# Row-wise log-softmax: stores moved to a second DMA queue, loads issued up to seven tiles ahead

## The chip, the cores and the metric

One core of one Trainium2 chip. The metric is the device time of one execution in microseconds (us), on the slowest core, which here is the only one. The granted clock was 1.0 in the profile of every run, and all runs were in the fast state.

## The reference

```python
x = randn(16, 512, 50000), float32
max_x = max(x, axis=-1);  shifted = x - max_x
out = shifted - log(sum(exp(shifted), axis=-1))
```

8192 rows of 50,000 numbers: 1638.4 MB are read once and 1638.4 MB written once.

## The kernel before

A tile is 16 whole rows, each cut into 8 pieces, so 128 partitions of 6250 numbers (25,000 B). There are 512 tiles and 8 buffers. A tile is loaded, reduced, exponentiated for its sum, scaled in place and stored from the same buffer.

```python
NBUF = 8
AHEAD = 5
...
    def load(t):
        buf = data.tile([P, W], FP32, name="buf")
        nc.sync.dma_start(out=buf, in_=xt[t])            # L75
...
    def front(t):
        nc.vector.reduce_max(out=pmax, in_=buf, axis=AX)  # L81
        ...                                  # row maximum over the 8 pieces -> negmax
        for j in range(nexp):                # 2 x 3125 columns, exp and its sum, L102
            nc.scalar.activation(out=dump, ..., func=ACT.Exp, bias=negmax[:, 0:1],
                                 accum_out=part[:, j : j + 1])
        ...                                  # TensorE sums the 8 pieces (L108), ScalarE takes Ln
    def back(t):
        nc.vector.tensor_scalar(out=buf, in0=buf, ...)    # L117, in place
        nc.sync.dma_start(out=ot[t], in_=buf)             # L121

    for t in range(AHEAD):
        load(t)
    for t in range(ntiles + 1):
        if t + AHEAD < ntiles:
            load(t + AHEAD)
        if t < ntiles:
            front(t)
        if t >= 1:
            back(t - 1)
```

The instructions of each engine run in the order of the program. Load k takes the buffer of tile k-8 and so waits for store k-8 to land, in this kernel and in the changed one.

## Time and profile before

| | before |
|---|---|
| time, median of 3 runs | 7904.5 us (7893.95 to 7905.24) |
| bytes moved | 3276.8 MB, 414 GB/s over the span |
| DMA busy share of its queue | 99.9% |
| VectorE busy | 5566.8 us (70%) |
| ScalarE busy | 3152.9 us (40%) |
| load, issue to landing | 23.5 us |
| store, issue to landing | 30.7 us |

Read the busy share with care. It says that DMA is the bound, not that DMA runs at its best: the share is 1.00 in the stage at 431 GB/s and in the stage at 406 alike. The GB/s row beside it is what tells the two apart. The prediction shows its lines.

### The profile page before, as it was taken

What the parts mean: (1) busy time and instruction counts of PE and PEld (TensorE: products, weight loads), DVE (VectorE), ACT (ScalarE), POOL (GpSimd) and SP (SyncE); (2) the same over time, 40 slices, a digit from 0 to 9 for tenths busy, and PEclk for the clock granted to TensorE, in tenths of its full rate; (3) what the DMA queues carried; (4) which work ended last, traced back from release to release, by engine and by line L of the source; (5) the groups of instructions that cost most, each with busy time, mean ns of one, the idle gap of its engine ahead of it and who ended that gap; (6) DMA issues with size and microseconds to landing.
All of it is one profiled execution on the core that took longest, in us unless ns stands there. A gap on an engine that the chain in (4) does not pass through costs nothing.

```text
span 7908.9 us, 12333 instructions
## 1 busy us (share of the span) xinstructions
PE 600.4 (8%) x2048; PEld 513.0 (6%) x2048; DVE 5566.8 (70%) x3072; ACT 3152.9 (40%) x2561; POOL 1.2 (0%) x7
## 2 busy tenths in 40 slices
PE   0000000000000000000000000000000000000000
PEld 0000000000000000000000000000000000000000
DVE  8777777777777776766666666766666666766665
ACT  4444444444444444333343434333343434333333
POOL 0000000000000000000000000000000000000000
DMA  9999999999999999999999999999999999999999
GB/s 416 426 430 431 431 431 431 431 431 431 431 430 431 429 428 410 410 403 409 409 406 403 404 405 408 407 408 405 409 408 401 406 403 413 408 405 406 406 405 385
DMA packets 147536, 3277.65 MB, mean 414 GB/s; under 512 B 16384, under 2 KB 16384, under 8 KB 16384
## 3 DMA queue, kind: packets, MB, share of 16 engines
q1 hardware_dynamic: 147456, 3276.87, 99.9%
q14 instruction: 64, 0.52, 0.0%
q8 instruction: 16, 0.26, 0.0%
HBM read 1638.40 MB, written 1638.40 MB: 414 GB/s over the span
## 4 chain that ended last, share of the span: by engine, by line
DMA 97%; SPq 1%; DVE 1%; issue 0%; ACT 0%; PE 0%; ACTq 0%
DMA out_dram<-buf 97%; SPq L75 1%; DVE pmax L81 1%; DMA buf<-in_x_dram 0%; DVE buf L117 0%; ACT dump L102 0%; DVE allmax L84 0%; DVE rowmax L86 0%; DVE spread L91 0%; DVE negmax L96 0%; PE rowsum L108 0%; ACT logsum L112 0%; ACTq L102 0%
## 5 line engine op out<-in xcount | busy, mean ns | idle before, releaser
L81 DVE TENSOR_REDUCE pmax<-buf 128x1 f32<-128x6250 f32 x512 | 3411.6, 6663 | 2231.9 <-DMA buf<-in_x_dram 2231.9
L102 ACT ACTIVATE dump<-buf,negmax 128x3125 f32<-128x3125 f32 x1024 | 2937.9, 2869 | 4370.9 <-DVE negmax L96 4354.4
L117 DVE TENSOR_SCALAR buf<-buf,negmax,logsum 128x6250 f32<-128x6250 f32 x512 | 1789.8, 3496 | 4.5 <-ACT logsum L112 3.6
L108 PE MATMUL rowsum<-part,ones 128*128 128x1 f32 x2048 | 600.4, 362 | 7269.8 <-ACT dump L102 7269.8
L108 PEld LDWEIGHTS rowsum<-part,ones 128*128 128x128 f32 x2048 | 513.0, 311 | 7357.1 <-ACT dump L102 7335.3
L112 ACT ACTIVATE logsum<-rowsum 128x1 f32<-128x1 f32 x512 | 87.8, 171 | 345.8 <-PE rowsum L108 345.8
L102 ACT ACTIVATION_READ_ACCUMULATOR dump<-buf,negmax 128x1 f32 x1024 | 190.8, 186 | 0.0
L96 DVE STREAM_TRANSPOSE negmax<-spread 128x32 f32<-128x32 f32 x512 | 108.2, 211 | 17.7
L84 DVE STREAM_TRANSPOSE allmax<-pmax 128x32 f32<-128x32 f32 x512 | 108.2, 211 | 17.5
L86 DVE TENSOR_REDUCE rowmax<-allmax 128x4 f32<-128x32 f32 x512 | 95.3, 186 | 17.8
L91 DVE COPY spread<-rowmax 128x32 f32<-128x32 f32 x512 | 92.9, 181 | 17.8
L67 ACT ACT_TABLE_LOAD x1 | 1.3, 1283 | 0.8 <-PEq L146 0.8
L59 POOL TENSOR_SCALAR_AFFINE_SELECT ones<-ones 128x128 f32<-128x128 f32 x1 | 0.4, 403 | 0.1
L63 POOL TENSOR_SCALAR_AFFINE_SELECT ones<-ones 128x128 f32<-128x128 f32 x1 | 0.4, 398 | 0.1
L57 POOL MEMSET ones<- 128x128 f32 x1 | 0.2, 204 | 0.3 <-POOLq L146 0.3
L146 POOL MEMSET const-bfloat16-1.0<- 128x1 bf16 x1 | 0.1, 102 | 0.0
L146 POOL MEMSET const-uint8-127<- 128x1 uint8 x1 | 0.1, 102 | 0.0
L146 POOL MEMSET const-float32-0.0<- 128x1 f32 x1 | 0.1, 99 | 0.3 <-issue 0.3
L146 POOL MEMSET const-float32-1.0<- 128x1 f32 x1 | 0.1, 99 | 0.0
## 6 DMA issues: line engine op xcount, KB each, us to landing
buf<-in_x_dram SPq DMA_DIRECT2D x512, 3125.0 KB, 23.5
out_dram<-buf SPq DMA_DIRECT2D x512, 3125.0 KB, 30.7
```

The lines of the kernel that those rows point to most:

```text
L59: nc.gpsimd.affine_select(out=ones3, in_=ones3, pattern=[[-G, R], [0, G]], base=0, channel_multiplier=1, compare_op=ALU.is_ge, fill=0.0,)
L67: nc.scalar.preload_act_table_set("natural_log_exp_and_others")
L75: nc.sync.dma_start(out=buf, in_=xt[t])
L81: nc.vector.reduce_max(out=pmax, in_=buf, axis=AX)
L84: nc.vector.transpose(out=allmax, in_=pmax.to_broadcast([P, SQ]))
L86: nc.vector.tensor_reduce(out=rowmax, in_=allmax.rearrange("p (r g) -> p r g", g=G), op=ALU.max, axis=AX, negate=True,)
L91: nc.vector.tensor_copy(out=spread.rearrange("p (r g) -> p r g", g=G), in_=rowmax[:, :, None].to_broadcast([P, SQ // G, G]),)
L96: nc.vector.transpose(out=negmax, in_=spread)
L102: nc.scalar.activation(out=dump, in_=buf[:, j * EXP_C : (j + 1) * EXP_C], func=ACT.Exp, bias=negmax[:, 0:1], scale=1.0, accum_out=part[:, ...
L108: nc.tensor.matmul(rowsum, ones, part[:, j : j + 1], start=j == 0, stop=j == nexp - 1)
L112: nc.scalar.activation(out=logsum, in_=rowsum, func=ACT.Ln)
L117: nc.vector.tensor_scalar(out=buf, in0=buf, scalar1=shift.pop(t)[:, 0:1], scalar2=logs.pop(t), op0=ALU.add, op1=ALU.subtract,)
```

## The change

The intent is that a load waiting for its buffer shall not hold up stores that are ready, and that loads run as far ahead as the buffers allow.

```diff
-AHEAD = 5
+AHEAD = 7
...
-        nc.sync.dma_start(out=ot[t], in_=buf)
+        nc.scalar.dma_start(out=ot[t], in_=buf)
...
     for t in range(ntiles + 1):
-        if t + AHEAD < ntiles:
-            load(t + AHEAD)
         if t < ntiles:
             front(t)
         if t >= 1:
             back(t - 1)
+        if t + AHEAD < ntiles:
+            load(t + AHEAD)
```

## The prediction

> **What bounds the kernel now.** I read the page from the slices down, then the waits, then a stretch of the timeline, then the trace's landing records. The slices first:
>
> ```profile
> DMA  9999999999999999999999999999999999999999
> GB/s 416 426 430 431 431 431 431 431 431 431 431 430 431 429 428 410 410 403 409 409 406 403 404 405 408 407 408 405 409 408 401 406 403 413 408 405 406 406 405 385
> ...
> q1 hardware_dynamic: 147456, 3276.87, 99.9%
> ...
> DMA 97%; SPq 1%; DVE 1%; issue 0%; ACT 0%; PE 0%; ACTq 0%
> ```
>
> The 16 DMA engines are busy 99.9% of the time and the chain that ended last is 97% DMA. So this is a transfer-bound kernel, and only two things can make it shorter: fewer bytes (the change moves the same 3276.87 MB) or more bytes per busy microsecond. The GB/s row is the clue: the same loop runs at 431 GB/s for fourteen slices and at some 406 for the rest. The table by stages says the same and clears the engines: DVE work stays about 69 to 73% busy, waiting in both.
>
> ```profile
> 1000.00:2000.00 1000.00, 78.74 (x269) 67.22 (x269) 728.63 (x402) 414.45 (x336) 0.00 (x0) 1.00 1.00 431
> 3400.00:4400.00 1000.00, 73.88 (x252) 63.11 (x252) 690.57 (x384) 388.95 (x316) 0.00 (x0) 1.00 1.00 406
> ```
>
> (Columns: length, busy us of PE, PEld, DVE, ACT, POOL; clock; DMA share; GB/s.) Who holds the DMA back? The queue's own waits, then one period of the timeline:
>
> ```profile
> SPq L75 <- DMA out_dram<-buf: 7333.8, 504, 23.6
> ```
>
> ```profile
> 1503.27 3.49 DVE L117 TENSOR_SCALAR buf<-buf,negmax,logsum 128x6250 f32<-128x6250 f32 x1
> 1503.29 0.33 SPq L75 DMA_DIRECT2D buf<-in_x_dram  x1
> 1503.66 0.46 SPq L121 DMA_DIRECT2D out_dram<-buf  x1
> 1510.60 6.66 DVE L81 TENSOR_REDUCE pmax<-buf 128x1 f32<-128x6250 f32 x1 [3.83 <-DMA buf<-in_x_dram]
> ```
>
> SyncE stands 7333.8 of 7908.9 us in front of a load, waiting for an old store to free its buffer. It is one in-order queue, so the next store stands behind that load: counting the scaling instructions (L117) done at each store issue, two later tiles are always already scaled when a store goes out. Those are buffers idle in SBUF. What is left in flight when a load is issued is only one load and one store, some 14.8 us of transfer.
>
> Now the part no view prints, from the trace's packets and its 16 landings per DMA (one per DMA engine). A 25,000 B row takes an engine 928 ns in both stages at the median; the loss is a tail. In the 500 us from 1500 us the mean packet is 931 ns, in those from 5000 us 983 ns, with 10% over 1.09 us. The long packets come in bursts that hit nearly all engines within 2 us. The gap from a DMA's first to its last landing, by tile: 1.2 us at the start, 4.6 at tile 20, 8.2 at 80, 11.7 at 140, 11.8 at 180, 13.5 from 220 to the end. One engine falls behind steadily, and at tile 300 the other fifteen lie within 2.6 us of each other with the last one 11.4 us behind them. A load's first landing comes 13.9 us after its issue at tile 100, but only 10.5 us at tiles 150 to 490; the very first load, into empty queues, takes 9.4 us. So from tile 150 on the leading engines have about 1 us of work left when the next load comes. That load needs the slowest engine's old store. The fifteen fast ones pile up at the end of their queue, restart together on every issue and change from load to store together, and then the bursts come. The same collective burst is there from 50 us on, when all engines are still in step from the start (411 GB/s at 60:80), and it fades as they drift apart. In between, spread out but not starved, nothing is lost.
>
> **What the Trainium skill says.** "DMA: Bandwidth & Descriptors", section "Where 436 GB/s comes from": 435 GB/s is the fabric's ceiling. The trace's 431 agrees; there is no room above the first stage. Section "Issuing engines are not separate DMA queues": queues of different issuers run on the same 16 engines and only issue time is saved. On that alone the change would be worth nothing; the trace of before has one busy queue, so cannot confirm it. Section "Queues, rings and completion order": each DMA engine round-robins between the queue rows that have work, packet by packet. If so, loads and stores will alternate row by row on each engine instead of eight rows of one and eight of the other; no run here shows it yet. Section "Latency and other measured facts": copies on the sync and scalar queues reach 214 GB/s per direction at full rate. That is 428 in total, within 1% of the 431 here, and speaks against a toll for alternating queues.
>
> **The change part by part.** Bytes, DMA count and all compute instructions stay.
> - Store issue moves from SyncE to ScalarE: 512 x 0.46 us = 235 us of ScalarE sequencer time. Per tile ScalarE has 2 x 2.87 + 2 x 0.19 + 0.17 = 6.3 us, and with the issue 6.8 of a 14.9 us period. Not on the path. The store follows the Ln of the next tile in program order; in the early timeline Ln ends 6.9 us after negmax and L117 3.4 us after it, so a store goes out some 3.5 us after it is ready. Against a queue tens of us deep that is hidden.
> - Stores no longer stand behind a waiting load. This removes the two scaled idle tiles. It does not remove the 7333.8 us of load wait: load t+7 now waits for store t-1, whose buffer it takes, and SyncE will still stand there nearly all the time.
> - AHEAD 7 with 8 buffers. At the issue of load t+7, a tile is held by compute from its landing until the next tile has landed (14.9 us), that one's maximum (6.66) and the small steps and exps (about 7.8): 29 us, two buffers. My estimate is that the other six are in DMA, as about two stores and four loads. Before the load counted in, that is five transfers x 7.4 = 37 us of backlog instead of 14.8.
> - What 37 us buys: the laggard lost 11.7 us over 140 tiles, 2100 us, so 5.6 ns per us. At that pace it needs 6600 us to drain the leaders, against 2200 before. The bunching then would come, if at all, at the very end. And if the engines do bunch, packet-wise alternation means no common change of direction. Both point the same way.
> - The sum: in the clean stage a tile takes 14.91 us by the slowest engine's landings (tiles 100 to 190), in the late stage 15.75 (250 to 490). All clean is 512 x 14.91 = 7633 us, plus about 10 us for first latency and the last tile's compute that no transfer covers: 7643. A few us of remaining bursts: 7650, or 3.2% below 7904.5.
>
> **Rivals.**
> 1. Hidden anyway. DMA is at 99.9% and the skill says that queues don't add bandwidth; if the 406 comes from addresses in HBM or from mere load/store mixing, the time stays at 7850 to 7950. For: busy share is full in both stages. Against: at tiles 50 to 180 the engines are already spread over most of a load and a store, so mixed, at 431; and the start shows the same bursts at other addresses, when in step.
> 2. A new bunching. With six tiles in DMA the slow engine still gates every load; if the fast ones starve earlier than my backlog says (for instance because the store queue runs dry and half of the loads are withheld), the late stage only starts later. At half of the lossy stage saved: 7904 - 130 = 7775, just within 2%.
> 3. A toll per change of queue. Sixteen changes per tile and engine instead of two. If each cost 50 ns, 16 x 0.05 x 512 = 410 us: 8050. For: in step, a common change costs about 0.5 us. Against: spread engines change direction with no loss in the clean stage (931 ns mean), and at the start the engines are already staggered over 0.8 us, nearly a whole packet.
> 4. ScalarE's in-order stores delaying exps: it has 8 us spare per tile, so I give this little.
>
> **Range and chances.** The floor is 1024 x 7.41 us (eight packets of 925 ns start to start and a 6 ns completion) = 7585, plus ends: not under 7595. The main case gives 7620 to 7700, rival 2 up to 7800, rival 1 up to 7930. I take 7650, with 7605 to 7910 for 8 in 10. Main case with part of rival 2: 0.66 for faster by over 2% (below 7746); rivals 1 and the rest of 2: 0.26 within 2%; rival 3: 0.08 slower.
>
> **What would show each step.** Two hardware queues with about half the bytes each; the GB/s row at 427 to 432 from the second slice to the 38th, with no step down; packets over 1 us nearly gone; in the landing records, a laggard allowed to fall over 20 us behind; SyncE still waiting for stores some 7000 us, but load and store landing times of about 40 to 70 and 20 to 40 us instead of 23.5 and 30.7, as the backlog is deeper; ScalarE waiting for L117 close to never. I am wrong in the mechanism if the row still falls to 406 in mid-run, if packets are longer everywhere, or if DMA share drops below 0.98, which would mean that the queues run dry.

## The result, and the profile after

| | before | after |
|---|---|---|
| time, median of 4 runs each | 7904.87 us (7893.95 to 7924.88) | 7614.22 us (7613.93 to 7616.07) |
| ratio of the fast runs | 1 | 0.963 (0.9611 to 0.9649) |
| GB/s over the span | 414 | 430 |
| load, issue to landing | 23.5 us | 51.9 us |
| store, issue to landing | 30.7 us | 37.5 us |

Ratios here are the mean time of one kernel's fast runs over that of the other's in the same rounds, so not quite the ratio of the medians. The change makes the kernel 3.7% faster. That lies inside the predicted range of 7605 to 7910 us but near its fast end: 36 us below the point forecast of 7650, and 6 us below the main case of 7620 to 7700.

The slices and the queues of the changed kernel:

```profile
DMA  9999999999999999999999999999999999999998
GB/s 425 433 432 432 432 432 432 432 432 432 432 432 432 432 432 432 432 432 432 432 432 432 432 432 432 432 432 432 432 432 432 432 432 432 431 432 432 432 432 380
...
q1 hardware_dynamic: 73728, 1638.43, 50.0%
q10 hardware_dynamic: 73728, 1638.43, 50.0%
```

The DMA row is what it was. The GB/s row has lost its step from 431 to some 406: it stands at 431 to 433 from the second slice to the last but one. Loads (q1) and stores (q10) share the DMA engines equally. The same two stages that the prediction compared, in the table by stages (columns as there), show DVE and ACT working at the same pace in both:

```profile
1000.00:2000.00 1000.00, 78.60 (x268) 67.17 (x268) 732.92 (x408) 413.22 (x336) 0.00 (x0) 1.00 1.00 432
3400.00:4400.00 1000.00, 79.20 (x270) 67.67 (x270) 729.10 (x403) 414.06 (x338) 0.00 (x0) 1.00 1.00 432
```

One period of the timeline, and SyncE's longest wait:

```profile
3001.49 0.34 ACTq L121 DMA_DIRECT2D out_dram<-buf  x1
3001.89 6.66 DVE L81 TENSOR_REDUCE pmax<-buf 128x1 f32<-128x6250 f32 x1 [3.83 <-DMA buf<-in_x_dram]
...
3009.41 3.50 DVE L117 TENSOR_SCALAR buf<-buf,negmax,logsum 128x6250 f32<-128x6250 f32 x1
```

```profile
SPq L75 <- DMA out_dram<-buf: 7305.6, 504, 26.8
```

SyncE waits for old stores as long as before (7333.8 us then), so that wait was never the cost. What has changed is what it holds up: only loads. A store now leaves on ScalarE's queue soon after its tile is scaled. DVE still waits 3.8 us a tile for a load.

The chain that ended last has to be read with care:

```profile
DVE 73%; another core or an unknown queue 25%; issue 1%; DMA 0%; ACT 0%; PE 0%; ACTq 0%
```

It seems to make VectorE the bound. But VectorE waits for a load in every tile, and the view lost the link at "unknown queue". The slices decide, not this line: the DMA engines are busy throughout, at the best rate that either kernel shows.

Where did the time go? By the landing records, load 195 has landed on all engines at 2882.0 us before and 2883.1 us after. By its loads, then, the changed kernel is level up to there. It is nevertheless ahead: by 2882 us the packet records have 1243.5 MB moved after and 1236.5 MB before. These 7.0 MB, two stores more, are some 16 us of transfer at 431 GB/s; nearly half of them are gained in the first 500 us. From load 195 to load 220, where the step comes in the kernel before, 17 us are gained; from load 220 to the last load 262 us (4585.9 against 4323.8); and from the last load to the end 18 us (52.2 against 33.7), because after the last load fewer stores are left to do: those of the start. With the 1.1 us lost earlier these make the 296 us between the two profiled spans.

The landing records also show how the engines lie apart. Each DMA lands 16 times, once per DMA engine. Mean over ten loads, us behind the first landing (columns: the 9th, 13th, 14th, 15th and 16th engine to land):

```
               tiles 100-109             200-209              480-489
before   2.7  5.5  5.6  5.8  9.2   1.2 2.3 3.6 6.2 13.0   1.1 1.8  2.0  2.2 13.5
after    1.9  2.4  3.7  5.7  6.3   1.3 2.2 6.5 8.9 10.8   5.5 6.7 22.1 27.3 30.3
```

In the kernel before, fifteen engines end up within 2.2 us of each other and one 13.5 us behind. In the changed one the last engine may fall 30 us behind and the rest stay spread out. How far an engine is behind the first is called its lag below. At the issue of a load, three loads and two stores are in flight in the changed kernel, one load and one store in the one before.

### The profile page after: what moved, and what is told of

It reads as the page before. It is cut to its first block, busy times and chain, and to the rows that moved or that the text cites. A ratio compares the mean times of both kernels' runs of the same rounds, so it can differ in the third digit from the quotient of the medians.

```text
span 7612.6 us, 12833 instructions
## 1 busy us (share of the span) xinstructions
PE 600.6 (8%) x2048; PEld 513.2 (7%) x2048; DVE 5567.2 (73%) x3072; ACT 3153.1 (41%) x2561; POOL 1.2 (0%) x7
## 4 chain that ended last, share of the span: by engine, by line
DVE 73%; another core or an unknown queue 25%; issue 1%; DMA 0%; ACT 0%; PE 0%; ACTq 0%
DVE pmax L81 45%; DVE buf L117 23%; DVE allmax L84 1%; DVE rowmax L86 1%; DVE spread L91 1%; DVE negmax L96 0%; DMA buf<-in_x_dram 0%; ACT dump L102 0%; PE rowsum L108 0%; ACT logsum L112 0%; ACTq L102 0%
## 5 line engine op out<-in xcount | busy, mean ns | idle before, releaser
L117 DVE TENSOR_SCALAR buf<-buf,negmax,logsum 128x6250 f32<-128x6250 f32 x512 | 1789.7, 3496 | 4.5 <-ACT logsum L112 3.6
## 6 DMA issues: line engine op xcount, KB each, us to landing
buf<-in_x_dram SPq DMA_DIRECT2D x512, 3125.0 KB, 51.9
out_dram<-buf ACTq DMA_DIRECT2D x512, 3125.0 KB, 37.5
```

The source lines that it names most:

```text
L117: nc.vector.tensor_scalar(out=buf, in0=buf, scalar1=shift.pop(t)[:, 0:1], scalar2=logs.pop(t), op0=ALU.add, op1=ALU.subtract,)
```

## The experiments

The theory has two parts. **Backlog:** a deep queue lets the DMA engines drift apart instead of running dry and restarting together. **Alternation:** with both queues full, each engine takes a row of a load and a row of a store by turns, so engines that do run together never change direction together after a long stretch. Either could suffice. "In step" means below that all 16 engines land a DMA within about 2 us. The rivals are the look-ahead itself, a plain gain by two queues, and a cause in the addresses. All kernels gave correct results. The times are medians of 4 runs; each ratio is to the fast runs of before of the same rounds, whose median was 7894.63 us for the first four experiments, 7898.99 for the next four and 7903.72 for the last.

### Experiment 1: the second queue alone

```diff
-        nc.sync.dma_start(out=ot[t], in_=buf)      # in the kernel before
+        nc.scalar.dma_start(out=ot[t], in_=buf)
```

> Stores on ScalarE, AHEAD and the loop order as before. Both theories agree: a load of tile k waits for the store of tile k-8 whatever AHEAD is, and with only loads in SyncE's queue the program order of loads against stores no longer matters. So 7614 us within 10, the GB/s row at 432 throughout. If AHEAD 7 itself carried part of the gain, this would be above 7700.

Measured 7614.16 us (7614.06 to 7614.32), ratio 0.9645. That is the changed kernel to 0.1 us, as expected. AHEAD 7 and the new place of the load add nothing: in a queue that holds only loads, each waits for its own buffer, whatever the loop says.

### Experiment 2: the look-ahead alone

```diff
-        nc.scalar.dma_start(out=ot[t], in_=buf)    # in the changed kernel
+        nc.sync.dma_start(out=ot[t], in_=buf)
```

> AHEAD 7 and the new loop order, but all DMA on SyncE. Load t+7 waits for store t-1, which was issued just before it, so the queue runs empty at each tile: one load from empty queues (10.2 us to its last landing at the start of before) plus one store (7.4 us) plus issue, some 18.4 us a tile, 9400 us (9200 to 9700). A theory that the look-ahead itself brings the gain would have it under 7750.

Measured 9726.94 us, ratio 1.232: 23% slower, and 27 us above the range expected. The period is 19.05 us, a little over the 18.4 expected. (The run keeps the new place of the load in the loop: in the old place, on one queue, load t+7 would wait for store t-1, which would stand behind it.) One queue makes a long look-ahead harmful, since each load waits for the store just ahead of it. One stage of it, by the table by stages, and its DMA issues:

```profile
1000.00:2000.00 1000.00, 61.66 (x211) 52.70 (x211) 571.22 (x318) 326.07 (x264) 0.00 (x0) 1.00 0.87 335
```

```profile
buf<-in_x_dram SPq DMA_DIRECT2D x512, 3125.0 KB, 11.4
out_dram<-buf SPq DMA_DIRECT2D x512, 3125.0 KB, 18.5
```

Here DMA really is idle for 13% of the time. All engines restart together at every tile (first to last landing of a load about 1.1 us), and this makes the run a clean place to measure the burst. I summed, over 158 tiles, how much longer than 928 ns the packets took (a packet record is here one row of 25,000 B, and 928 ns its median), per engine and tile, by the time since the load's issue:

```
us since the load's issue     0 to 3   3 to 7   7 to 10   from 10   sum
experiment 2                  0.745    0.014    1.061     0.006     1.83
before, 4500 to 6500 us       0.200    0.160    0.487     0.026     0.87
before, 1500 to 2700 us                                             0.06
after, 4500 to 6500 us                                              0.01
```

In experiment 2 the load's rows run from 1 to 9 us and the store's from there on. So the long packets sit at two places: where the load starts on empty queues, and where all engines go from load to store (1.06 us). In between, with sixteen engines side by side, there is nothing.

The two differ in kind. The kernel before loses 0.82 us per engine in its first 5 us, with loads alone, so a start on empty queues costs about as much as the 0.745 without any change of direction. And a new DMA that all engines begin in step is not dear in itself: from 5 to 51 us the first seven loads of the kernel before run back to back, in step, and lose 0.03 us in all. Its first change from load to store, from 51 to 56 us, costs 0.76 us.

The late stage of the kernel before has bursts at the same times, and its 0.87 - 0.06 = 0.81 us explains the growth of its period from 14.91 to 15.75 us.

### Experiment 3: one queue, a deeper backlog

```diff
-AHEAD = 5      # in the kernel before
+AHEAD = 4
```

> The kernel before with AHEAD 4: still one queue, so no alternation of rows, but a load now waits for an older store, with four transfers (29.7 us) still in flight instead of two (14.8). Backlog theory: the last engine may fall some 26 us behind before the others run dry, so the step down comes only in the last third or not at all, 7650 to 7720 us. Alternation theory (two queues protect because each DMA engine mixes loads and stores row by row): no gain, 7850 to 7950 with the step at about 2900 us.

Measured 7674.07 us (7667.96 to 7689.77), ratio 0.9724: the backlog theory's number. Its GB/s row:

```profile
GB/s 416 426 430 430 430 431 430 431 432 431 431 430 431 431 431 431 431 431 431 431 431 431 431 431 431 431 431 431 430 431 430 430 431 427 416 410 416 410 420 361
```

The step is still there but has moved from slice 15 to slice 34 (counted from 0). In the landing records the last engine falls behind to some 26 us, the limit that was forecast, stays near there from tile 352 on, and the loss comes some 80 tiles later, when the others have closed up. So the addresses are not the cause: the same tiles move at 431 GB/s in this run and at 406 in the kernel before. And a loop that looks *less* far ahead is better here, because a load then waits for an older store. Counted as the prediction counts, no later tile stands scaled when a store goes out (two did in the kernel before).

### Experiment 4: two queues, a shallow backlog

```diff
-NBUF = 8       # in the changed kernel
-AHEAD = 7
+NBUF = 5
+AHEAD = 4
```

> The changed kernel with 5 buffers (AHEAD 4): two queues, rows alternate, but only about two transfers in flight at a load's issue, as in the kernel before. Backlog theory: engines bunch when the last one is some 11 us behind, and the step down from 432 to about 407 comes back, 7800 to 7950 us. Alternation theory: the engines bunch but no common change of direction follows, 7610 to 7680 us with the GB/s row flat.

Measured 7622.05 us (7621.23 to 7627.42), ratio 0.9657, the alternation theory's number. Its GB/s row and DMA issues:

```profile
GB/s 425 432 432 432 432 432 432 432 432 432 431 432 430 430 429 432 431 431 430 431 431 431 431 429 431 431 431 431 428 431 432 432 431 430 430 431 431 430 429 405
...
buf<-in_x_dram SPq DMA_DIRECT2D x512, 3125.0 KB, 22.2
out_dram<-buf ACTq DMA_DIRECT2D x512, 3125.0 KB, 22.6
```

With five buffers there are again one load and one store in flight at a load's issue, and a load lands 22.2 us after it, as in the clean stage of before. The lag is pinned from tile 128 on, at some 8 to 9.5 us. Twelve engines close up to within 3 us, and three stragglers stay well behind them. In the kernel before, a picture not far from it (twelve within 1.8 us, at 3000 us) already cost 3 to 5% of the rate. Here it costs 0.06 us a tile. So a backlog as shallow as before's is enough with two queues. The bunching was not as complete as in the late stage of before: a load's first landing comes 13.8 us after its issue, against 10.5 there, so the leading engines still had some 3 us more to do. That alternation is what protects this run is therefore argued here and not shown, which is why experiment 7 follows.

### Experiments 5 and 6: do instruction fetches make the stragglers?

In the changed kernel's records, two of the three stragglers lose 0.7 to 1.0 us at a time, at moments when a packet of instructions goes over the core's DMA engines (the records do not say over which one). So I lengthened TensorE's instruction stream threefold, once in each kernel.

```diff
+        for _ in range(3):
             for j in range(nexp):
                 nc.tensor.matmul(rowsum, ones, part[:, j : j + 1], ...)
```

> The kernel before with its matmuls done three times over (same result, TensorE far from busy), so that TensorE's instruction stream is three times as long. Fetch theory: DMA engines fall behind because they also fetch instructions (in the changed kernel's landing records two of the three stragglers step back by 0.7 to 1.0 us at the times of instruction packets); with three times the TensorE fetches its engine falls behind two to three times as fast, the step down comes at about 1200 to 1700 us instead of 2900, and the time is 7960 to 8030. If the straggling has nothing to do with fetches: step at 2900 us, 7890 to 7930.

> The changed kernel with its matmuls done three times over. Fetch theory: one engine's lag reaches the backlog's end (some 30 us) about half way, after that all run at the straggler's pace, 7640 to 7690 us. If bunched engines then lost time as in the kernel before, it would be over 7750 with a step down to about 407 GB/s; if alternation protects, the GB/s row stays at 428 to 431 to the end. Without an effect of fetches: 7614.

Experiment 5 measured 7892.81 us (7850.06 to 7935.03 over 20 runs), ratio 0.9987: no effect, a miss. Its row steps down in the same slice:

```profile
GB/s 419 427 429 430 431 430 431 430 431 431 430 430 430 429 429 417 417 414 411 408 413 404 412 413 412 408 405 405 411 409 407 407 410 405 407 407 408 406 408 389
```

Experiment 6 measured 7628.76 us (7623.86 to 7629.55), ratio 0.9647, between the two forecasts. The effect exists but is a third of what I had taken: the longer stream had 48 instead of 16 fetches of 16 KB, and at tiles 288 to 297 the last engine lagged 21.2 us instead of 15.7. By then 18 fetches had been added, so each costs the last engine an estimated 0.31 us (5.5 us over 18). The lag of the others did not change (9.8 and 13.1 against 9.5 and 12.6). In the one-queue kernel the lag is pinned early in any case, and the loss begins only when the other engines have closed up, which these fetches do not hasten.

### Experiment 7: two queues that run dry

```diff
-NBUF = 8       # in the changed kernel
-AHEAD = 7
+NBUF = 4
+AHEAD = 3
```

> The changed kernel with 4 buffers: hardly anything in flight at a load's issue, so the engines restart together at every tile, with two queues. Alternation theory: idle time appears, but the packets stay short, mean under 945 ns (with one queue and all engines in step, the run with all DMA on SyncE and AHEAD 7, the mean was 1042 ns); 7650 to 7900 us. If rows alternating do not protect, mean over 970 ns and over 7950 us.

Measured 8172.02 us, ratio 1.0333, mean packet 977 ns. By the letter of what I had written, alternation failed. The trace shows why, and it is the best evidence for it. With four buffers one queue is often empty, so both a pure stretch and an alternating one occur, with all engines in step (first to last landing 0.7 us at the median for loads). Two windows of its DMA view, 4042 to 4048 us and 4022 to 4027 us:

```profile
q1 hardware_dynamic: 49, 1.23, 48.5%
q10 hardware_dynamic: 49, 1.23, 47.4%
```

```profile
q10 hardware_dynamic: 92, 1.90, 90.0%
q1 hardware_dynamic: 11, 0.00, 0.1%
```

Rows started per microsecond in the packet records, and how much they exceeded 928 ns (us per engine):

```
us after 4000     23   24   25   26   27  | 43   44   45   46   47   48
loads (q1)         0    0    0    0    0  |  1   15    1   15    1   15
stores (q10)      16   16   16   16   16  | 15    1   15    1   15    1
excess          0.00 0.05 0.00 0.03 0.79  | 0    0    0    0    0    0
```

On the right all sixteen engines change direction together, from load to store and back, every 0.93 us, and the excess is zero to the hundredth. On the left they have been storing since 21 us, then loads come in behind them (at 28 us), and 0.79 us is lost at that one change. A common change of direction is free after one row and dear after a long stretch. The two windows are no exception. I cut the packet records of this run from 200 to 8000 us into slices of 0.93 us, one row each, and summed the excess over the two slices before each change of direction and the one after it (a slice has a direction when over 90% of its rows have it). Some 1880 changes after a single slice lose about 0.02 us each, 202 after 7 to 9 slices of stores about 0.8 us, and 206 after 6 to 8 slices of loads about 0.5 us. The changed kernel shows the same at its start, where its engines are still nearly in step (2 us from first to last landing). Its first change, at 34 to 37 us after loads alone, costs 0.76 us; from 38 to 80 us, where loads and stores alternate and often twelve of the sixteen engines start the same direction together, it loses 0.002 us in all. Alternation protects as long as both queues hold work; the expected mean below 945 ns failed because I had not seen that four buffers leave them empty by turns.

### Experiment 8: fewer instructions

```diff
-EXP_C = 3125   # in the changed kernel; dump in PSUM, float32
-NBUF = 8
-AHEAD = 7
+EXP_C = 6250   # dump in SBUF, bfloat16
+NBUF = 7
+AHEAD = 6
```

> The changed kernel with one exp of 6250 columns a tile (dump in SBUF as bf16, 7 buffers), which halves TensorE's instructions and cuts ScalarE's. Fetch theory: the second and third straggler, now 27 and 22 us behind at the end, are some 10 to 18 us behind; the last one, whose lag grows smoothly, is not explained by fetches and stays at about 25 to 31 us, so the time stays at 7605 to 7620.

Measured 7612.14 us (7610.58 to 7612.96), ratio 0.9627. This is the fastest version of all, but by 2 us of 7614; it is no reason to change the kernel. The lags at tiles 480 to 489 are 14.6, 22.6 and 24.9 us instead of 22.1, 27.3 and 30.3. So all three shrink: the nearest as expected, the second less than expected, and the last, which was to stay at 25 to 31, to just below that. (The larger dump also costs a buffer, so two loads and two stores are in flight at a load's issue instead of three and two.) Fetches are part of the lag and not the whole: in the changed kernel, between fetches, the last engine still loses some 0.04 us a tile (median, tiles 60 to 490), and no record shows why.

### Experiment 9: one queue, deeper still

```diff
-AHEAD = 5      # in the kernel before
+AHEAD = 3
```

> One queue, AHEAD 3: a load now waits for the store of five tiles back, so up to six transfers are queued, less some 11 us in which a store waits for compute: about 33 us of backlog. Backlog theory: the straggler (26 us after 5500 us with AHEAD 4) meets the limit of about 30 us only near the end, so there is no step down before the last tenth: 7635 to 7665 us, some 20 to 40 us above the changed kernel because the start in step still costs and packets are 931 ns instead of 928. If two queues were needed for a clean run, over 7700.

Measured 7646.35 us (7644.06 to 7649.66), ratio 0.9679. The row has no step:

```profile
GB/s 416 426 429 430 431 430 431 431 431 431 431 431 431 431 431 431 431 431 431 430 431 431 431 431 431 431 431 431 431 431 431 431 431 431 431 431 431 431 430 375
```

At a load's issue three loads and three stores are in flight, and the last engine lags 31 us at the end without meeting a limit. One constant in the kernel before, turned the other way, brings 257 of the 291 us. Most of the rest is the start in step (416 and 426 in the first two slices against 425 and 433) and packets of 931 instead of 928 ns.

## Why the prediction was right

**The bound.** Right. DMA stays busy, SyncE still waits 7305.6 us ("some 7000"), and the gain is all in GB/s. That there is no room above the first stage was right too, at 432 GB/s, though the section cited for the ceiling goes on to say that for transfers between HBM and SBUF the HBM side binds, at about 358 GB/s per core. The prediction passed over that; this program on one core, at 431 and 432 GB/s, decides against it here.

**The step down as bunching, not addresses.** Right. Up to load 195 the loads of the two kernels land level, and what the changed one gains there is some 16 us of stores, about half of them from the start; the step down is the rest. Experiments 3 and 9 move the step or remove it, with the same addresses and the same single queue.

**Two protections.** The backlog is confirmed without the other by experiment 9 (7646 us with one queue). That engines in step change direction freely row by row is confirmed by experiment 7 and by the start of the changed kernel; that this alone carries a whole run is likely from experiment 4 (7622 us with a shallow backlog), though its engines were not fully bunched. The text treated the two as pointing the same way, without saying which one does the work. In the changed kernel the backlog never ran out (at tiles 480 to 489 a load's first landing still comes 21.8 us after its issue, against 9.4 on empty queues), so its mid-run does not test alternation; its start does. Even the shallow experiment 4 is 24 us faster than the deepest one-queue kernel (medians of other rounds, on another chip).

**Row by row.** Right, with some luck. The prediction read the "packet" of the Trainium skill's page "DMA: Bandwidth & Descriptors", section "Queues, rings and completion order", as one row. That section gives a packet as typically 9 to 17 descriptors and does not speak of rows of 25,000 B; a switch after eight rows would have fitted its words as well, and would have left long stretches of one direction. Experiment 7 shows the switch after each row.

**Five transfers of backlog.** Right: three loads and two stores in flight. But the text put this under "AHEAD 7 with 8 buffers". That attribution was wrong: experiment 1 has it with AHEAD 5. The backlog comes from stores no longer standing behind a waiting load, which the prediction had named as a separate part.

**The lag's pace.** 5.6 ns per us were taken from the kernel before; the changed kernel lost 30.3 us by tiles 480 to 489, about 7150 us, so 4.2 ns per us. The leaders did not run dry. (The pace before was read with the start in step in it. The records give 0.8 us at the start and some 4 at tile 20, where the prediction has 1.2 and 4.6.)

**The time.** 7650 forecast, 7614 measured. The mis-sized term is the period of a clean tile: 14.91 us was read from before's clean stage, and the changed kernel has 14.86 us (tiles 250 to 490), which over 512 tiles is 26 us. Before's clean stage was not quite clean: its packets averaged 931 ns, here 928.4. All one-queue runs stay at 931 ns and 14.91 us at their best (experiments 3 and 9 too); why was not tried. The other two terms were too large as well: the ends took some 7 us and not 10, and the "few us of remaining bursts", 7 in the sum, did not come: past the start, the excess is 0.01 us a tile. The three make the 36 us. (In the floor, 1024 x 7.41 is 7588 and not 7585; nothing rests on that.)

**The rivals.** "Hidden anyway" fell with the GB/s row. "A new bunching" did not occur within the run. "A toll per change of queue" is measured in experiment 7 as nothing for alternating rows. The 214 GB/s that the prediction set against it could not decide this: the same page has them from copies between HBM tensors and does not say that the rows of two queues alternated there. ScalarE's stores in front of the exps: in the period shown the store leaves at 3001.49 us, 0.06 us after the Ln starts, and the list of ScalarE's waits over the whole run has none for L117.

**Landing times.** 51.9 and 37.5 us lie in the ranges given (40 to 70, 20 to 40).

**What stays open.** Why a common change of direction after a long stretch, or a common start on empty queues, costs 0.5 to 1 us, in memory or in the fabric, was not tried; only when it happens is shown. Why one engine lags beyond its fetches is open too.

## What to carry to other kernels

When DMA is 100% busy, look at GB/s over time before calling it the floor: a step in that row at unchanged work was 3% of the time here. Put loads that wait for a buffer and stores that are ready into different queues, and keep both filled, so that each DMA engine mixes the two directions row by row; if there is only one queue, let a load wait for an old store, not a young one. Looking further ahead is not the same as having more in flight: with one queue, AHEAD 7 was 23% slower than AHEAD 5 and AHEAD 3 was 3% faster.

## What the Trainium skill lacked or had wrong

- "DMA: Bandwidth & Descriptors", section "Issuing engines are not separate DMA queues": it says that issuing from several engines only saves the sequencer's time. Here issue time lay off the path and a second queue alone (experiment 1) brought 3.6%, because it ended the blocking of ready stores and made rows alternate; 3.2% can be had on one queue, too (experiment 9). It is right in that the peak is the same, 431 against 432 GB/s.
- The same page, section "Queues, rings and completion order": that each engine round-robins between queues, packet by packet, agrees with the trace. The grain that it gives, typically 9 to 17 descriptors from one queue before the switch, does not tell what to expect of rows like these: here it is one row of 25,000 B (0.93 us) from each queue by turns (experiment 7).
- No page that I read says that a single queue of loads and stores can fall from 431 to 406 GB/s at a busy share of 99.9%. Nor has one the cost of all DMA engines changing direction together after a long stretch: 1.06 us a tile from load to store in experiment 2, about 0.02 us a change when they change after every row (experiment 7).
- No page that I read says how far the 16 DMA engines of one core drift apart within a kernel on the queues of SyncE and ScalarE (31 us after some 480 tiles, experiment 9), nor that a shallow queue then ties all of them to the last one.
- No page that I read has what an instruction fetch costs the DMA engine it passes through: an estimated 0.31 us for 16 KB in experiment 6, and 0.7 to 1.0 us at the times of the 8 KB packets in the changed kernel.
